# The end of the mixers in a hand-made order, and a first up chunk made of two parts

## The chip, the cores and the metric

The kernel runs on 1 core of one Trainium2 chip. The metric is device time in microseconds (us) of one execution, the median of 3 runs.

## The reference

One inference step of a decoder layer, for 256 prompt tokens and 8 x 4 sampled tokens (288 in all), width 1024, in float32:

```
h   = RMSNorm(x)
p   = h @ w_in                       # columns [q | k | v | B | C | u]
att = rotary q/k, dilated sliding-window attention, 8 heads of 64
cnv = B * causal_depthwise_conv3(C * u)          # 512 channels
mix = concat(RMSNorm(att), RMSNorm(cnv)) @ w_out
x  += RMSNorm(mix)
x  += RMSNorm(relu(RMSNorm(x) @ w_up)^2 @ w_down)
```

Outputs are the new x, the new keys and values, and the convolution's state (the last two rows of C * u, `o_cs` in the kernel).

## The kernel before, in words

**Layout.** Activations lie transposed: 128 channels on the partitions, 288 tokens along a row. A width of 1024 is eight such blocks ("rows" here, index `kc` or `j`). The weights come in 96 chunks, each the eight 128x128 blocks that make 128 output channels: chunks 0 to 7 are q and k, 8 to 11 v, 12 to 23 C, u and B of the convolution, 24 to 31 `w_out` (outputs `mix0` to `mix7`), 32 to 63 `w_up`, 64 to 95 `w_down`. SyncE's queue brings them in blocks of two (`raw`, line 137) into three buffers; a block is requested when the buffer of the third block before it is free.

**Two-part floats.** A float32 product is made of three passes over rounded parts. ACT writes the high part `hi` of a chunk (L164), DVE or POOL the rest `lo` (L165, `split_w`), into three buffers (`splp`) and two more (`spx`). Activations have the same two parts: `mh` and `ml` (attention half `mh0`, `ml0`, convolution half `mh1`, `ml1`), later `hh` and `hl`. `mm3` (L198) issues hi·xh, hi·xl and lo·xh, so that a chunk is 24 matmuls of 288 columns. `take` and `ahead` split a chunk one ahead of its use.

**The end of the mixers.** The gated convolution makes four channel blocks `co`. For the last two, TensorE makes B (chunks 22 and 23), DVE multiplies (`bs2`, `bs3`, then `co`), ACT squares (`sqc`), and `rsqrt_rows` (L205) sums the squares with a matmul (`ss_conv`), takes logarithm and exponential on ACT, and mends the result on DVE (L214, L215, L218). Meanwhile five chunks of `w_out` (`NW = 5`) run over the four rows of the attention half, `mix_half(m, 0, True)`. Then each of the five runs over the convolution half, and mix5, mix6, mix7 are whole chunks. POOL makes `lo24` and `lo25` (`POOL_LO`) and `ml1` of the second convolution row (`POOL_ML`).

**From the mix to the up product.** `post` (L715) squares each mix output (`q_m`, summed in `ssm`) and scales it with the gain of the norm (`mg`). After mix7 comes the norm (`ss_mix`, `y_mix`, `t_mix`, `s1`), and TensorE runs 28 filler matmuls (`warm(WARM1)`, L243) whose result is not used. Then DVE and ACT make row by row mg·s1, the new x, `hh` = x·g and `hl`. Row 0 has a short cut: `gx` = x·g of row 0 and `gm`, which is mix0 times both gains, are made early, and hh0 = gm·s1 + gx. Four up chunks (`NW = 4`) follow the rows as they come; after them each up chunk runs by itself, and `evac_up` (L795 to L798) writes the squared relu into `fh` and `fl`.

**What sets the order.** A scheduler orders the instructions of each engine by the order in which the program text issues them, its estimates, and the hints `after`, `issue_after` and `high_priority`. Inside `manual_schedule` the named engines take the order of the text. Every engine and DMA queue takes its instructions in order; semaphores make it wait for what others write.

Of the kernel before, what the change touches and what calls it, by code (L numbers as in the profile page):

```python
# [108 lines left out]
def layer(ctx, tc, xt, vec, cst, kt, vt, st, wts, o_y, o_k, o_v, o_cs):  # L109
# [483 lines left out]
    def group_norm(src, vcol, c0, c1, hf, ssq, nm, pool, tag):  # L593
        n = c1 - c0
        if mh[hf] is None:
            mh[hf] = act.tile([P, 4, NT], F32R, tag="act", name=f"mh{hf}")
            ml[hf] = act.tile([P, 4, NT], F32R, tag="act", name=f"ml{hf}")
        dh, dl = mh[hf], ml[hf]
        s = nrm.tile([P, NT], F32, tag="s", name=f"s_{nm}")
        if n <= 64:  # L600
            for ch in range(4):
                nc.scalar.mul(src[:, ch, c0:c1], src[:, ch, c0:c1], vv[:, vcol + ch:vcol + ch + 1])
        chain = rsqrt_rows(ssq, m512, n, s[:, :n], nm, pool, tag)
        if n <= 64:
            nc.vector.tensor_mul(src[:, :, c0:c1], src[:, :, c0:c1], s[:, :n].unsqueeze(1).to_broadcast([P, 4, n]))
            nc.scalar.copy(dh[:, :, c0:c1], src[:, :, c0:c1])
            d = nc.vector.tensor_sub(dl[:, :, c0:c1], src[:, :, c0:c1], dh[:, :, c0:c1].bitcast(F32))
            return chain[0], d.ins
        for ch in range(4):
            nc.vector.scalar_tensor_tensor(src[:, ch, c0:c1], src[:, ch, c0:c1], vv[:, vcol + ch:vcol + ch + 1],  # L610
                                           s[:, :n], ALU.mult, ALU.mult)
            nc.scalar.copy(dh[:, ch, c0:c1], src[:, ch, c0:c1])
            e = nc.gpsimd if hf == 1 and ch in POOL_ML else nc.vector
            e.tensor_sub(dl[:, ch, c0:c1], src[:, ch, c0:c1], dh[:, ch, c0:c1].bitcast(F32))
# [42 lines left out]
    group_norm(aT, V_ATT, 0, SEQ, 0, [acc_a[:, 0:SEQ]], "attp", pa, "a")  # L657
# [8 lines left out]
    picks = d_select(1)  # L666
    b2 = conv_b(2, 22, [lambda: [f() for f in picks[0:2]], lambda: [f() for f in picks[2:4]]])
    es.close()
    pt = ctx.enter_context(tc.tile_pool(name="pt", bufs=6, space=PSUM))
    spx = ctx.enter_context(tc.tile_pool(name="spx", bufs=2, side="right"))  # L670
    sqd = cv.tile([P, 4, ND], F32, tag="w", bufs=4, name="sqd")
    acc_d = cv.tile([P, ND], F32, name="acc_d")
    with tc.high_priority():
        nc.scalar.square(sqd, aT[:, :, SEQ:NT])
        d = nc.vector.tensor_reduce(acc_d, sqd.rearrange("p c t -> p t c"), axis=mybir.AxisListType.X, op=ALU.add)
        chain = group_norm(aT, V_ATT, SEQ, NT, 0, [acc_d], "attd", pt, "o")
# [3 lines left out]
    b3 = conv_b(3, 23)  # L680
    sq3 = cv.tile([P, NT], F32, tag="w", bufs=4, name="sqc3")
    with tc.high_priority():
        conv_out(*b3)
# [1 line left out]
        with after(last_mm[0]):
            group_norm(co, V_CONV, 0, NT, 1, [acc_c, sq3], "conv", pt, "o")
    NW = 5
    ws = [take(24, 0)]
    with after(*chain[:1]):
        ws += [take(25, 0)] + [split_w(26 + m, parts=4, pool=spx) for m in range(2)] + [take(28, 0)]  # L690
    pss = []

    def mix_half(m, hf, start):
        if start:
# [1 line left out]
        for j in range(4):
            mm3(pss[m][:, :NT], ws[m], 4 * hf + j, mh[hf][:, j], ml[hf][:, j], start and j == 0, not start and j == 3)

    for m in range(NW):
        mix_half(m, 0, True)  # L700
# [70 lines left out]
    with tc.manual_schedule(engines={mybir.EngineType.DVE, mybir.EngineType.Activation}):  # L771

        nc.vector.tensor_mul(gm, gm, s1)
        nc.vector.tensor_add(hh[0][:, 0], gm, gx)
# [3 lines left out]
        low_h(0)
        for kc in range(2, KC):
            residual(kc)  # L780
            hi_last = high_h(kc)
            low_h(kc - 1)
        lo_last = low_h(7)
        residual(0)
# [16 lines left out]
    pss = [pt.tile([P, 512], F32, tag="o", name=f"up{m}") for m in range(NW)]  # L801
    for kc in range(2):
        for m in range(NW):
            mm_h(pss[m][:, :NT], ws[m], kc, hh[0][:, kc], kc == 0)
        for m in range(NW):
            mm_l(pss[m][:, :NT], ws[m], kc, hl[0][:, kc], False)
    for kc in range(2, KC):
        for m in range(NW):
            mm3(pss[m][:, :NT], ws[m], kc, hh[kc // 4][:, kc % 4], hl[kc // 4][:, kc % 4], False, kc == KC - 1)
# [111 lines left out]
```

## Time and profile before

| | |
|---|---|
| time, median of 3 runs | 380.72 us (380.51 to 380.85) |
| profiled execution, its own time | 380.2 us |
| its span, first to last instruction | 378.4 us |
| mean granted TensorE clock | 0.99 |
| busy: TensorE, weight loads | 363.9 us (96%), 336.3 us (89%) |
| busy: DVE, ACT, POOL | 230.1 us (61%), 195.8 us (52%), 32.1 us (8%) |
| DMA | 76.23 MB, mean 201 GB/s |

The span is one profiled execution, 1.8 us shorter than that execution's own time. PE is TensorE, PEld its weight loads (beside the matmuls), DVE, ACT and POOL are VectorE, ScalarE and GpSimd, SP is SyncE. L205 is line 205 of the kernel before. Matmuls are pipelined, so the durations of neighbours overlap; the distance of their starts is their pace. Names are those of the program without their numbers: `hi` stands for every chunk's high part. A row's bracket tells how long the engine had been idle and what released it.

### The profile page before, as it was taken

What the parts mean: (1) busy time and instruction counts of PE and PEld (TensorE: products, weight loads), DVE (VectorE), ACT (ScalarE), POOL (GpSimd) and SP (SyncE); (2) the same over time, 40 slices, a digit from 0 to 9 for tenths busy, and PEclk for the clock granted to TensorE, in tenths of its full rate; (3) what the DMA queues carried; (4) which work ended last, traced back from release to release, by engine and by line L of the source; (5) the groups of instructions that cost most, each with busy time, mean ns of one, the idle gap of its engine ahead of it and who ended that gap; (6) DMA issues with size and microseconds to landing.
All of it is one profiled execution on the core that took longest, in us unless ns stands there. A gap on an engine that the chain in (4) does not pass through costs nothing.

```text
span 378.4 us, 6776 instructions
## 1 busy us (share of the span) xinstructions
PE 363.9 (96%) x2722; PEld 336.3 (89%) x2722; DVE 230.1 (61%) x421; ACT 195.8 (52%) x368; POOL 32.1 (8%) x58
## 2 busy tenths in 40 slices
PE   8999999999999999999999999999999999999971
PEld 7899688676886899899999999999999999999960
DVE  3889767447394967698876666666434344434417
ACT  5979537343364767355765555555344334433310
POOL 0005100114323300000000000000000000000012
PEclk9999999999999999999999999999999999999996
DMA  7994799987993436504535353535444444542003
GB/s 210 423 407 199 263 408 418 409 322 272 396 395 125 133 107 236 193 3 132 203 112 212 124 197 138 186 149 177 158 164 171 153 181 138 197 129 95 2 0 125
DMA packets 18079, 76.23 MB, mean 201 GB/s; under 512 B 2048, under 2 KB 8448, under 8 KB 11136
## 3 DMA queue, kind: packets, MB, share of 16 engines
q1 hardware_dynamic: 17040, 74.56, 53.3%
q10 hardware_dynamic: 1008, 1.24, 0.9%
q8 instruction: 21, 0.34, 0.4%
q14 instruction: 10, 0.08, 0.1%
HBM read 73.40 MB, written 2.40 MB: 200 GB/s over the span
## 4 chain that ended last, share of the span: by engine, by line
PE 85%; DVE 8%; ACT 2%; DMA 2%; issue 1%; SPq 1%; POOL 1%; DVEq 0%; ACTq 0%; POOLq 0%
PE dn L201 9%; PE dn L203 9%; PE dn L202 9%; PE up L201 8%; PE up L203 8%; PE up L202 8%; PE d L470 3%; PE dpv L514 2%; PE mix L201 2%; PE mix L202 2%; PE mix L203 2%; PE qk L203 2%; DMA raw<-wts 2%; PE qk L201 2%; PE qk L202 2%; PE u L201 1%
## 5 line engine op out<-in xcount | busy, mean ns | idle before, releaser
L165 DVE TENSOR_TENSOR lo<-raw,hi 128x1024 fp32r<-128x1024 f32 (+1 forms) x99 | 112.1, 1140 | 78.1 <-ACT hi L164 77.9
L164 ACT CAST hi<-raw 128x1024 fp32r<-128x1024 f32 (+1 forms) x104 | 97.7, 950 | 97.7 <-PE dn L202 56.6
L201 PE MATMUL dn<-fh,hi 128*128 128x288 f32 x256 | 75.8, 296 | 0.0
L202 PE MATMUL dn<-fl,hi 128*128 128x288 f32 x256 | 75.6, 295 | 0.0
L203 PE MATMUL dn<-fh,lo 128*128 128x288 f32 x256 | 75.3, 294 | 0.0
L202 PE MATMUL up<-hl,hi 128*128 128x288 f32 x248 | 73.4, 296 | 0.0
L201 PE MATMUL up<-hh,hi 128*128 128x288 f32 x248 | 73.1, 296 | 0.0
L203 PE MATMUL up<-hh,lo 128*128 128x288 f32 x248 | 73.0, 294 | 0.0
L203 PEld LDWEIGHTS dn<-fh,lo 128*128 128x128 f32 x256 | 48.2, 188 | 0.0
L202 PEld LDWEIGHTS dn<-fl,hi 128*128 128x128 f32 x256 | 48.1, 188 | 0.0
L201 PEld LDWEIGHTS dn<-fh,hi 128*128 128x128 f32 x256 | 48.0, 188 | 0.0
L203 PEld LDWEIGHTS up<-hh,lo 128*128 128x128 f32 x248 | 46.7, 188 | 0.1
L202 PEld LDWEIGHTS up<-hl,hi 128*128 128x128 f32 x248 | 46.6, 188 | 0.1
L201 PEld LDWEIGHTS up<-hh,hi 128*128 128x128 f32 x248 | 46.4, 187 | 0.0
L795 DVE SCALAR_TENSOR_TENSOR r<-up,s 128x288 f32<-128x288 f32 x32 | 14.2, 456 | 14.1 <-PE up L203 14.0
L834 POOL TENSOR_TENSOR mg<-mg,y_f 128x288 f32<-128x288 f32 x1 | 1.0, 1008 | 232.2 <-ACT y_f L213 232.2
L201 PE MATMUL mix<-mh,hi 128*128 128x288 f32 x64 | 19.3, 302 | 0.0
L202 PE MATMUL mix<-ml,hi 128*128 128x288 f32 x64 | 19.0, 297 | 0.0
L203 PE MATMUL mix<-mh,lo 128*128 128x288 f32 x64 | 18.9, 295 | 0.0
L798 DVE TENSOR_TENSOR fl<-r,fh 128x288 fp32r<-128x288 f32 x32 | 14.0, 451 | 0.0
L797 ACT CAST fh<-r 128x288 fp32r<-128x288 f32 x32 | 13.3, 430 | 0.7
L796 ACT ACTIVATE r<-r 128x288 f32<-128x288 f32 x32 | 13.6, 439 | 0.0
(242 smaller groups left out, 636.3 us busy)
## 6 DMA issues: line engine op xcount, KB each, us to landing
raw<-wts SPq DMA_DIRECT2D x45, 1024.0 KB, 4.9
k<-kt SPq DMA_DIRECT2D x16, 640.0 KB, 11.4
v<-vt SPq DMA_DIRECT2D x9, 1024.0 KB, 11.1
raw<-wts SPq DMA_DIRECT2D x4, 512.0 KB, 8.8
o_y<-mg SPq DMA_DIRECT2D x8, 144.0 KB, 1.8
v<-vt SPq DMA_DIRECT2D x2, 512.0 KB, 11.1
c<-cst SPq DMA_DIRECT2D x1, 838.0 KB, 9.4
...
```

The lines of the kernel that those rows point to most:

```text
L164: a = nc.scalar.copy(hi[:, cs], raw[:, cs])
L165: b = (eng or nc.vector).tensor_sub(lo[:, cs], raw[:, cs], hi[:, cs].bitcast(F32))
L201: nc.tensor.matmul(ps, lhsT=a, rhs=xh, start=start, stop=False)
L202: nc.tensor.matmul(ps, lhsT=a, rhs=xl, start=False, stop=False)
L203: return nc.tensor.matmul(ps, lhsT=lo[:, j * P:(j + 1) * P], rhs=xh, start=False, stop=stop)
L470: nc.tensor.matmul(ps[32 * i:32 * i + 32, 0:n], lhsT=qbd[:, p, 4 * g + i], rhs=t[:, i, 0:n], start=p == 0, stop=p == 3, tile_position=(0, ...
L514: nc.tensor.matmul(dpv[g][32 * i:32 * i + 32], lhsT=pt[:, j, 32 * i:32 * i + 32], rhs=t[i], start=False, stop=j == 4, tile_position=(0, 32 ...
L795: nc.vector.scalar_tensor_tensor(r, ps[:, :NT], 0.0, s2, ALU.max, ALU.mult)
L796: nc.scalar.square(r, r)
L797: nc.scalar.copy(fh[:, m], r)
L798: nc.vector.tensor_sub(fl[:, m], r, fh[:, m].bitcast(F32))
L834: nc.gpsimd.tensor_mul(mg[:, 0], mg[:, 0], y)
```

## The change

On the attention half nothing changes but its order. From the B product of chunk 22 to the last convolution-half matmul of the first five mix chunks, TensorE, DVE and ACT now take the order of the text (`manual_schedule`). In it:

- Every split is whole or in two parts, on DVE (before: quarters for chunks 25 to 28, and POOL for `lo24`, `lo25` and one `ml`).
- mix0 and two rows of mix1 come before the sums `ss_conv`. The convolution half of the five chunks runs row by row over all five for two rows, then chunk by chunk for the last two.
- `hi29` is written before the first square of the mix outputs, and the DMA of `o_cs`, on ACT's queue, is issued behind it.

The fillers after mix7 go. In their place, chunk 32, the first of `w_up`, is computed in two parts from what is known before the norm: since the new x is x + s1·mg, its six rows 0 to 5 (`NS = 6`) give `up0a` = w·(x·g) and `up0b` = w·(mg·g), and up0 = up0a + s1·up0b. Each part has 18 matmuls. Nine run before the sums of the norm, 27 after them. The twelve rows x·g and mg·g get high and low parts on ACT and DVE (`apart`), stored in rows 20 to 31 of `fh` and `fl`. Rows 6 and 7 of chunk 32 run after the norm like before. The order of rows is now 6, 7, 0 to 5, with the short cut (`gx`, `gm`) on row 6. The first block has five up chunks (`NW = 5`), chunk 36 is split before the norm, and two DVE operations on `bs1` put up0 together.

The core of the diff (`rsqrt_rows`, `post`, `residual` and `high_h` stay as they were):

```
-    def group_norm(src, vcol, c0, c1, hf, ssq, nm, pool, tag):
...
+    with tc.manual_schedule(engines={mybir.EngineType.PE, mybir.EngineType.DVE, mybir.EngineType.Activation}):
+        ahead(23)
+        ahead(24)
+        ys = [conv_y(ch) for ch in (2, 3)]
...
+        w25 = high_w(25, splp)
...
+        sq_add(acc_c, co[:, 2], "sqc2", False)
+        low_w(25, w25)
+        b3 = g_in(23, "B3")
+        ws = [take(24, 0), w25] + [high_w(26 + i, spx) for i in range(2)]
+        conv_out(3, b3, ys[1])
...
+        nc.scalar.square(sq3, co[:, 3])
+        ws.append(high_w(28, splp))
+        low_w(26, ws[2])
+        low_w(27, ws[3])
+        low_w(28, ws[4], 0, 512)
...
+        mix_rows(0, 0, range(4))
+        mix_rows(1, 0, range(2))
+        s_c = nrm.tile([P, NT], F32, tag="s", name="s_conv")
+        rsqrt_rows([acc_c, sq3], m512, NT, s_c, "conv", pt, "o")
...
+        mix_rows(1, 0, range(2, 4))
+        for m in range(2, NW):
+            mix_rows(m, 0, range(4))
+        for j in range(2):
+            for m in range(NW):
+                mix_rows(m, 1, [j])
+        for m in range(NW):
+            mix_rows(m, 1, range(2, 4))
+        ahead(29)
...
-    nc.scalar.dma_start(out=o_cs, in_=cst_t)
+    with tc.issue_after(splits[29][0]):
+        nc.scalar.dma_start(out=o_cs, in_=cst_t)
...
+    def apart(i, kc, src):
+        g = vv[:, V_MPRE + kc:V_MPRE + kc + 1]
+        a, b = parts[i][kc], parts[i][NS + kc]
+        nc.scalar.mul(a, src, g)
+        nc.vector.scalar_tensor_tensor(b, src, g, a.bitcast(F32), ALU.mult, ALU.subtract)
+
+    for kc in range(NS):
+        apart(0, kc, x[:, kc])
     for m in range(8):
...
         last = post(ps, m, V_POST, mg[:, m], ssm, "m")
-        if m == 0:
+        if m < NS:
+            apart(1, m, mg[:, m])
+        elif m == NS:
             nc.scalar.mul(gm, ps[:, :NT], vpp)
...
-    rsqrt_rows([ssm, last], m1024, NT, s1, "mix")
-    warm(WARM1, "mix", last)
+    w0 = take(32, 0)
+    apsum = [pt.tile([P, 512], F32, tag="o", name=f"up0{n}") for n in "ab"]
+
+    def product(i, kc):
+        mm3(apsum[i][:, :NT], w0, kc, parts[i][kc], parts[i][NS + kc], kc == 0, i == 1 and kc == NS - 1)
+
+    with tc.manual_schedule(engines={mybir.EngineType.PE}):
+        for kc in range(3):
+            product(0, kc)
+        rsqrt_rows([ssm, last], m1024, NT, s1, "mix")
+        for i, kc in [(0, kc) for kc in range(3, NS)] + [(1, kc) for kc in range(NS)]:
+            product(i, kc)
...
+            if i == 3:
+                nc.vector.tensor_mul(bs1, apsum[1][:, :NT], s1)
...
-    ws = [take(32 + m, 0) for m in range(2)] + [split_w(34 + m, pool=spx) for m in range(2)]
+    ws = [w0, take(33, 0)] + [split_w(34 + m, pool=spx) for m in range(2)] + [take(36, 0)]
     with tc.issue_after(hi_last), tc.issue_after(lo_last):
-        ahead(36)
+        ahead(37)
...
+        if m == 0:
+            with tc.issue_after(lo_last):
+                nc.vector.tensor_add(bs1, ps[:, :NT], bs1)
+            ps = bs1
...
-    NW = 4
...
+    NW = 5
+    pss = apsum[:1] + [pt.tile([P, 512], F32, tag="o", name=f"up{m}") for m in range(1, NW)]
+    for i, kc in enumerate(order):
+        ms = range(0 if kc >= NS else 1, NW)
```

How the instructions stand on two engines. On DVE, around `bs3`, the first product of the last convolution block (`co` in its rows is the output, `t_conv` begins the norm's mending steps). Before:

```order
L591 TENSOR_TENSOR acc_c_1404<-acc_c_1404,sqc2_1613 128x288
L605 TENSOR_TENSOR aT_177<-aT_177,s_attd_1591 128x4x32
L607 TENSOR_TENSOR ml0_1406<-aT_177,mh0_1405 128x4x32
L165 TENSOR_TENSOR lo26_1692<-raw13_258,hi26_1691 128x256
L573 TENSOR_TENSOR bs3_1650<-B3_1624,s0_170 128x288
L165 TENSOR_TENSOR lo26_1692<-raw13_258,hi26_1691 128x256
L574 TENSOR_TENSOR co_670<-bs3_1650,cv3_1616 128x256
L576 TENSOR_TENSOR co_670<-bs3_1650,cv3_1616 128x28
L578 TENSOR_TENSOR co_670<-bs3_1650,cv3_1616 128x4
```

And now:

```order
L697 TENSOR_TENSOR ml0_1406<-aT_177,mh0_1405 128x4x32
L604 TENSOR_TENSOR acc_c_1404<-acc_c_1404,sqc2_1625 128x288
L178 TENSOR_TENSOR lo25_1620<-raw12_256,hi25_1619 128x1024
L586 TENSOR_TENSOR bs3_1660<-B3_1629,s0_170 128x288
L587 TENSOR_TENSOR co_670<-bs3_1660,cv3_1550 128x256
L589 TENSOR_TENSOR co_670<-bs3_1660,cv3_1550 128x28
L591 TENSOR_TENSOR co_670<-bs3_1660,cv3_1550 128x4
L178 TENSOR_TENSOR lo26_1655<-raw13_258,hi26_1654 128x1024
```

The quarters of `lo26` that stood before and behind `bs3` are gone; the whole `lo25`, which was POOL's, stands in front of it, and `lo26` behind the three products.

On ACT, from the mix outputs to the split of chunk 31 (`hi31`), which mix7 multiplies. Before:

```order
L720 ACTIVATE q_m1_1836<-mix1_1734 128x288
L721 ACTIVATE mg_1800<-mix1_1734,vv_95 128x288
L164 CAST hi30_1892<-raw15_262 128x1024
L720 ACTIVATE q_m2_1852<-mix2_1747 128x288
L721 ACTIVATE mg_1800<-mix2_1747,vv_95 128x288
L720 ACTIVATE q_m3_1868<-mix3_1760 128x288
L721 ACTIVATE mg_1800<-mix3_1760,vv_95 128x288
L164 CAST hi31_1925<-raw15_262 128x1024
L720 ACTIVATE q_m4_1884<-mix4_1773 128x288
```

And now (`fh` is the high part of a row of x·g or mg·g):

```order
L162 CAST hi30_1890<-raw15_262 128x1024
L767 ACTIVATE gx_1846<-x_94,vv_95 128x288
L775 ACTIVATE fh_1842<-x_94,vv_95 128x288 x6
L756 ACTIVATE ssm_1844<-mix0_1673 128x288
...
L775 ACTIVATE fh_1842<-mg_1841,vv_95 128x288 x2
...
L757 ACTIVATE mg_1841<-mix4_1677,vv_95 128x288
L756 ACTIVATE q_m5_1919<-mix5_1894 128x288
L775 ACTIVATE fh_1842<-mg_1841,vv_95 128x288
L757 ACTIVATE mg_1841<-mix5_1894,vv_95 128x288
L162 CAST hi31_1925<-raw15_262 128x1024
L775 ACTIVATE fh_1842<-mg_1841,vv_95 128x288
```

`hi31` stood behind the scaled copy of mix3; it now stands behind that of mix5, with `gx`, the six copies of x and five of `mg` ahead of it.

On ACT, further on, from mix7 to the logarithm of the norm (`y_mix`). Before:

```order
L164 CAST hi32_2054<-raw16_264 128x1024
L164 CAST hi33_2058<-raw16_264 128x1024
L720 ACTIVATE q_m6_1954<-mix6_1929 128x288
L721 ACTIVATE mg_1800<-mix6_1929,vv_95 128x288
L720 ACTIVATE q_m7_1983<-mix7_1958 128x288
L721 ACTIVATE mg_1800<-mix7_1958,vv_95 128x288
L212 ACTIVATE y_mix_1994<-ss_mix_1991,epsc_120 128x288
```

And now:

```order
L162 CAST hi32_1992<-raw16_264 128x1024
L162 CAST hi33_2087<-raw16_264 128x1024
L162 CAST hi34_2091<-raw17_266 128x1024
L162 CAST hi35_2095<-raw17_266 128x1024
L756 ACTIVATE q_m7_1984<-mix7_1959 128x288
L757 ACTIVATE mg_1841<-mix7_1959,vv_95 128x288
L162 CAST hi36_2099<-raw18_268 128x1024
L221 ACTIVATE y_mix_2012<-ss_mix_2009,epsc_120 128x288
```

`hi34` and `hi35`, which stood ahead of mix5's square, and `hi32` and `hi33` now stand directly ahead of the square of mix7, and `hi36` between that and the logarithm.

## Rows read from the trace of the kernel before

**Rows 1.** The page's busy time of each engine (share of the span, instructions)

```profile
PE 363.9 (96%) x2722; PEld 336.3 (89%) x2722; DVE 230.1 (61%) x421; ACT 195.8 (52%) x368; POOL 32.1 (8%) x58
```

**Rows 2.** TensorE's waits: us in total, times, longest

```profile
PE up L196 <- DVE hl L767: 0.4, 1, 0.4
```

**Rows 3.** TensorE's timeline: start us, us, instruction, count, idle before and releaser

```profile
128.96 0.75 PE L209 MATMUL ss_conv<-sqc,m 128*128 128x288 f32 x2 [0.85 <-ACT sqc L684]
129.68 0.29 PE L202 MATMUL mix<-ml,hi 128*128 128x288 f32 x1
...
153.53 0.65 PE L209 MATMUL ss_mix<-ssm,m 128*128 128x288 f32 x2
...
154.78 3.29 PE L243 MATMUL warm_mix<-q_m,m 128*128 128x128 f32 x28
158.47 0.40 PE L192 MATMUL up<-hh,hi 128*128 128x288 f32 x1 [0.40 <-DVE hh L774]
...
162.42 0.56 PE L201 MATMUL up<-hh,hi 128*128 128x288 f32 x3
```

**Rows 4.** Timeline of POOL and DVE while `lo25` is split

```profile
123.70 3.25 POOL L165 TENSOR_TENSOR lo<-raw,hi 128x256 fp32r<-128x256 f32 x4 [3.23 <-ACT hi L164]
126.28 0.95 DVE L165 TENSOR_TENSOR lo<-raw,hi 128x256 fp32r<-128x256 f32 x1
127.52 0.41 DVE L165 TENSOR_TENSOR lo<-raw,hi 128x256 fp32r<-128x256 f32 x1
```

**Rows 5.** ACT's timeline

```profile
10.48 0.96 ACT L236 ACTIVATE xh<-x,vv 128x288 fp32r<-128x288 f32 x2
...
137.60 1.05 ACT L164 CAST hi<-raw 128x1024 fp32r<-128x1024 f32 x1 [0.37 <-PE mix L202]
138.55 0.41 ACT L720 ACTIVATE ssm<-mix 128x288 f32<-128x288 f32 x1
138.85 0.49 ACT L721 ACTIVATE mg<-mix,vv 128x288 f32<-128x288 f32 x1
139.24 0.50 ACT L742 ACTIVATE gm<-mix,vpp 128x288 f32<-128x288 f32 x1
...
143.99 1.05 ACT L164 CAST hi<-raw 128x1024 fp32r<-128x1024 f32 x1 [0.65 <-PE mix L202]
...
153.73 0.41 ACT L720 ACTIVATE q_m<-mix 128x288 f32<-128x288 f32 x1 [1.58 <-PE mix L203]
...
154.98 0.50 ACT L212 ACTIVATE y_mix<-ss_mix,epsc 128x288 f32<-128x288 f32 x1 [0.45 <-PE ss_mix L209]
...
159.31 0.54 ACT L756 ACTIVATE hh<-x,vv 128x288 fp32r<-128x288 f32 x1 [3.35 <-DVE x L753]
...
168.87 0.78 ACT L760 ACTIVATE q_x<-x 128x288 f32<-128x288 f32 x2
```

**Rows 6.** DVE's timeline

```profile
145.07 1.23 DVE L165 TENSOR_TENSOR lo<-raw,hi 128x1024 fp32r<-128x1024 f32 x1 [1.52 <-ACT hi L164]
146.71 2.36 DVE L165 TENSOR_TENSOR lo<-raw,hi 128x1024 fp32r<-128x1024 f32 x2
...
155.99 0.46 DVE L214 SCALAR_TENSOR_TENSOR t_mix<-y_mix 128x288 f32<-128x288 f32 x1 [2.92 <-ACT y_mix L213]
```

**Rows 7.** The page's DMA issues: count, KB each, us to landing

```profile
raw<-wts SPq DMA_DIRECT2D x45, 1024.0 KB, 4.9
...
o_cs<-cst_t ACTq DMA_DIRECT2D x1, 36.0 KB, 1.5
```

**Rows 8.** SyncE's timeline: the request for chunks 36 and 37

```profile
146.33 0.33 SPq L137 DMA_DIRECT2D raw<-wts  x1
```

**Rows 9.** The tail in TensorE's timeline

```profile
366.28 0.65 PE L842 MATMUL sum<-x,ident 128*128 128x288 f32 x2
...
371.81 1.33 PE L847 MATMUL sum<-mg,ident 128*128 128x288 f32 x2 [4.88 <-DVE mg L845]
```

**Rows 10.** Windows of the tail: busy (count) PE PEld DVE ACT POOL, clock, DMA

```profile
371.00:372.00 1.00, 0.19 (x1) 0.19 (x2) 1.00 (x2) 0.00 (x0) 1.00 (x2) 0.52 0.20 70
```

More of the change, by code (lines that the diff above doesn't have):

```diff
@@ L169, in layer, with raw_of, high_w, low_w @@
     splits = {}
+    def raw_of(s):
+        return blocks[s // 2][:, (s % 2) * 1024:(s % 2) * 1024 + 1024]
+    def high_w(s, pool):
+        w = [pool.tile([P, 1024], F32R, tag=n, name=f"{n}{s}") for n in ("hi", "lo")]
+        nc.scalar.copy(w[0], raw_of(s))
+        return w
+    def low_w(s, w, a=0, z=1024):
+        nc.vector.tensor_sub(w[1][:, a:z], raw_of(s)[:, a:z], w[0][:, a:z].bitcast(F32))
     def after(*ins):
@@ L181, in ahead @@
         if s < 96 and s not in ready:
-            ready[s] = split_w(s, parts=4 if s in (1, 2) or 25 <= s <= 28 else 1, eng=nc.gpsimd if s in POOL_LO else None)
+            ready[s] = split_w(s, parts=4 if s in (1, 2) else 1)
     def take(s, n=1):
@@ L591, in sq_add, with prompt_norm @@
             (e or nc.vector).tensor_add(acc, acc, t[:, :n])
-    def group_norm(src, vcol, c0, c1, hf, ssq, nm, pool, tag):
[L594 to L608, printed above, removed]
-        for ch in range(4):
[L610 to L614, printed above, removed]
+    def prompt_norm():
+        for i in range(2):
+            mh[i] = act.tile([P, 4, NT], F32R, tag="act", name=f"mh{i}")
+            ml[i] = act.tile([P, 4, NT], F32R, tag="act", name=f"ml{i}")
+        s = nrm.tile([P, NT], F32, tag="s", name="s_attp")
+        rsqrt_rows([acc_a[:, 0:SEQ]], m512, SEQ, s[:, :SEQ], "attp", pa, "a")
+        for ch in range(4):
+            a, h = aT[:, ch, 0:SEQ], mh[0][:, ch, 0:SEQ]
+            nc.vector.scalar_tensor_tensor(a, a, vv[:, V_ATT + ch:V_ATT + ch + 1], s[:, :SEQ], ALU.mult, ALU.mult)
+            nc.scalar.copy(h, a)
+            nc.vector.tensor_sub(ml[0][:, ch, 0:SEQ], a, h.bitcast(F32))
     v_chunk(0)
@@ L656, in layer @@
     acc_c = cv.tile([P, NT], F32, tag="acc", name="acc_c")
[L657 removed]
+    prompt_norm()
     conv_c(3, 20)
@@ L665, in layer @@
         sq_add(acc_c, co[:, ch], f"sqc{ch}", ch == 0, nc.gpsimd)
[L666 to L676, printed above, removed]
@@ L677, in layer @@
-    with after(chain[0], d.ins):
-        conv_out(*b2)
-        sq_add(acc_c, co[:, 2], "sqc2", False)
[L680 to L683, printed above, removed]
-        nc.scalar.square(sq3, co[:, 3])
[L685 to L690, printed above, removed]
@@ L691, in layer, with mix_rows @@
-    pss = []
-    def mix_half(m, hf, start):
-        if start:
-            pss.append((pg if m < 2 else pt).tile([P, 512], F32, tag="g" if m < 2 else "o", name=f"mix{m}"))
[L696 to L700, printed above, removed]
+    ahead(22)
+    NW = 5
+    pss = []
+    def mix_rows(m, hf, js):
+        for j in js:
+            mm3(pss[m][:, :NT], ws[m], 4 * hf + j, mh[hf][:, j], ml[hf][:, j], hf == 0 and j == 0, hf == 1 and j == 3)
@@ L771, in layer @@
     with tc.manual_schedule(engines={mybir.EngineType.DVE, mybir.EngineType.Activation}):
+        order = list(range(NS, KC)) + list(range(NS))
         nc.vector.tensor_mul(gm, gm, s1)
-        nc.vector.tensor_add(hh[0][:, 0], gm, gx)
-        residual(1)
-        hi_last = high_h(1)
+        nc.vector.tensor_add(hh[NS // 4][:, NS % 4], gm, gx)
+        residual(order[1])
+        hi_last = high_h(order[1])
         nc.vector.tensor_add(gx, gm, gx)
[L778 to L784, printed above, removed]
-    ws = [take(32 + m, 0) for m in range(2)] + [split_w(34 + m, pool=spx) for m in range(2)]
+        low_h(NS)
+        for i in range(2, KC):
+            residual(order[i])
+            hi_last = high_h(order[i])
+            low_h(order[i - 1])
+            if i == 3:
+                nc.vector.tensor_mul(bs1, apsum[1][:, :NT], s1)
+        lo_last = low_h(order[7])
+        residual(NS)
+    ws = [w0, take(33, 0)] + [split_w(34 + m, pool=spx) for m in range(2)] + [take(36, 0)]
     with tc.issue_after(hi_last), tc.issue_after(lo_last):
-        ahead(36)
+        ahead(37)
         for kc in range(KC):
@@ L798, in evac_up @@
         nc.vector.tensor_sub(fl[:, m], r, fh[:, m].bitcast(F32))
-    NW = 4
[L801 to L809, printed above, removed]
+    NW = 5
+    pss = apsum[:1] + [pt.tile([P, 512], F32, tag="o", name=f"up{m}") for m in range(1, NW)]
+    for i, kc in enumerate(order):
+        ms = range(0 if kc >= NS else 1, NW)
+        a, b = hh[kc // 4][:, kc % 4], hl[kc // 4][:, kc % 4]
+        for m in ms:
+            mm_h(pss[m][:, :NT], ws[m], kc, a, i == 0 and m > 0)
+            if i > 1:
+                mm_l(pss[m][:, :NT], ws[m], kc, b, i == (KC - 1 if m else KC - NS - 1))
+        if i < 2:
+            for m in ms:
+                mm_l(pss[m][:, :NT], ws[m], kc, b, m == 0 and i == KC - NS - 1)
     for m in range(NW, 32):
         w = take(32 + m)
-        ps = (pg if m == 6 else pt).tile([P, 512], F32, tag="g" if m == 6 else "o", name=f"up{m}")
+        ps = (pg if m == 5 else pt).tile([P, 512], F32, tag="g" if m == 5 else "o", name=f"up{m}")
         last = gemm(ps, w, hh, hl)
```

51 lines of the change are left out of this document (41 added, 10 removed).

## The prediction

> **What bounds the kernel now.** I read the busy shares first. TensorE is busy for 363.9 of 378.4 us [rows 1], so a change can win only where TensorE stands, or where it does work that can go. I then read TensorE's waits: inside the stretch that the change touches they are short, such as 0.4 us for the first low part of the up product [rows 2]. The timeline shows the others [rows 3]: 0.85 us for the conv square before `ss_conv`; and from 154.78 to 158.47 TensorE does only the filler `warm_mix`, while the norm of the mix output runs on ACT and DVE. The reader is to see there also the pace: from the second matmul after the conv wait, 129.68, to the last norm, 153.53, stand 179 matmuls of 288 columns, 0.1333 us each. A chunk (24 of them) costs 3.20 us, so mix4 ended at 143.94 and mix6 at 150.33.
>
> The other engines are asked only for what must be ready. ACT's timeline [rows 5] gives prices by start-to-start time: 0.95 for a `hi` cast of 1024 columns (137.60 to 138.55), 0.30 for a square out of PSUM, 0.39 for a scaled copy out of PSUM. Two scaled copies from SBUF, `xh<-x,vv`, take 0.96 and one alone 0.54, so each further one costs 0.42. ACT takes its instructions in the written order.
>
> **Part 1, the end of the mixers.** The wait of 0.85 us at 128.96 [rows 3] has its cause on DVE: `sqc3` needs the last conv output, and DVE reached it late, behind quarter splits. One of these took 0.95 us while POOL was splitting lo25 (123.70 to 126.95), the next 0.41 [rows 4]. The change takes lo24, lo25 and one `ml` from POOL and puts them whole on DVE. That is 1.18 us for each `lo` (two in 2.36, [rows 6]): lo24 goes into DVE's idle time before `om`, lo25 stands directly before `bs3`. DVE loses the slowed quarter and its halves around `bs3`, so `bs3` starts at about the same time. TensorE gets six matmuls more to do before it needs `sqc3` (two rows of mix1), 6 x 0.1333 = 0.80 us, nearly the wait's length. I take 0.80 us gained here. Bounds: 0, if lo25 holds `bs3` back, for which mix1 now waits because it reuses its PSUM buffer; 1.1, if POOL's silence shortens the small DVE operations as well. The nearest row is the wait itself. In after's second half the chunks go side by side, and each ends six matmuls (0.80) after the one before: mix0 at 139.94, mix2 at 141.54, mix4 at 143.14, mix6 at 149.54.
>
> **Part 2, what ACT now has before hi31.** Here the price lies. Before, mix0 to mix4 ended 1.6 us apart and ACT did each chunk's square and scaled copy as it came; hi31 started at 143.99, as soon as its buffer came free [rows 5]. In the new row order hi31 stands behind everything that chunks 0 to 5 leave on ACT. Followed by price: the square of mix2 starts 0.2 us after mix2 ends (the latency of the square of mix7, 153.53 to 153.73 [rows 3, 5]), at 141.74; hi30 at 142.04; `gx` at 142.99. (`gx` also waits for `o_cs`, now issued behind hi29; hi29 can start at 139.94, so with 1.5 us to landing [rows 7] it is there by 142.4.) From `gx` to hi31 stand 12 scaled copies from SBUF (`gx`, six parts of x, five of `mg`): 12 x 0.42 = 5.04; six `mg`: 6 x 0.39 = 2.34; four squares: 4 x 0.30 = 1.20. The sum is 8.58, so hi31 starts at 151.57 and ends 1.05 later, at 152.62. DVE's lo31 takes 1.23 [rows 6]: 153.89.
>
> TensorE is through with mix6 at 149.54. It stands until 152.6, does the two matmuls that need hi31 alone, and stands again until 153.93 for lo31. The 22 matmuls left of mix7 end at 156.86, where 152.74 was to be had. That is a stand of 4.1 us, new and not in any row of before.
>
> The same queue goes on. From hi31's start 0.95; part 5 0.42; the square of mix6 0.30; `mg` and `gm` 0.78; hi32 to hi35 4 x 0.95 = 3.80: the square of mix7 starts at 157.82, though mix7 was over at 156.86. After it and `mg` (0.69) stands hi36, at 158.51. Its block (chunks 36 and 37) is requested only when lo31 has released the buffer (before: lo31 ended at 146.30, the request went out at 146.33 [rows 6, 8]), so at 153.9, and lands 4.9 later [rows 7], at 158.8. hi36 ends at 159.88, lo36 then holds DVE for 1.18, and only behind it stands the norm's first DVE step `t_mix`: 161.1 against 155.99 [rows 6]. The logarithm and exponential on ACT (159.8 to 160.8) are ready before that. From `t_mix` to the first up matmul were 2.48 us before (155.99 to 158.47), the same steps now: 163.6. So TensorE gets there 5.1 us later.
>
> **Part 3, the two-part first up chunk.** It adds 36 matmuls ahead of that point, in place of the 28 fillers. Nine run from 156.86 to 158.1, before the norm's sums (about 1.2 us), 27 after these, to about 163: hidden whole. Of the 768 up matmuls (32 chunks), 18 need not run after the norm: 18 x 0.1333 = 2.40 us won. If they were not hidden (a norm that came back as early as before) up to 1.2 us of them would show. The first two rows serve five chunks instead of four, 15 matmuls instead of 12. Before, the first 24 matmuls (3.20) took from 158.47 to 162.42 [rows 3], 0.75 us lost; now one wait of some 0.4 for the first `hl` is left: 0.3 won. The two additions on `bs1` (0.46 each at `t_mix`'s price) lie on DVE beside TensorE, which needs 1.6 us for a row of twelve where DVE needs about 1.3. Were that cover gone they would cost 0.9.
>
> **Sum.** +5.1 - 2.4 - 0.3 = +2.4 us, the 0.8 of part 1 being inside the 5.1. Against the profiled execution's own 380.2 us that is 382.6. Its 380.2 is 0.5 below the median of the runs, 380.72, so I forecast **383.1 us**.
>
> Bounds of the terms. The twelve scaled copies may cost 0.34 (two squares `q_x` from SBUF take 0.78, one 0.44) to 0.54 (one alone): -1.0 to +1.4 us. I keep 0.42, the same operation with the same shapes. Part 1: +0.8 to -0.3. A landing of the block 0.5 us later or earlier moves `t_mix` by +0.5 or -0.3, the queue on ACT being then last.
>
> **The clock.** In the tail TensorE stands for 4.88 us; there the granted clock falls from 1.00 to 0.52, that is from 2.4 to 1.2 GHz, and the same pair of matmuls takes 1.33 instead of 0.65 us [rows 9, 10]. The new stand is 3.1 us, two matmuls, 1.0 us. No row of before has one of that length. If the clock fell there, the 22 matmuls of mix7 would cost 2.9 us more; 0.8 of that hides, because ACT takes up mix7's square only 0.8 us after it may. The Trainium skill (TensorE: Matmul & The Clock Gate, Part 1) says that half rate is the array's default and full rate is held only while the array is busy; by that rule the removal of the fillers and this stand speak against the change, and the sum would be the rival's below, not mine.
>
> **Rivals.**
> - ACT keeps up (faster). If hi31 were ready at 149.5, mix7 would end at 152.74, nine products and the sums would end at about 155.2, `t_mix` would start some 0.2 us after 155.99, and 2.7 us are won: 378.2 us. It decides at 6.5 us for the list that I price at 8.58 (142.99 to 149.54): the scaled copies would have to cost 0.25 each. No ACT row of 288 columns is below 0.30. For it speaks only that one execution's profile was read. Chance 0.13.
> - Gain and stand cancel. Copies at 0.34, POOL's silence worth the full 1.1, the block early: 2.4 - 1.0 - 0.3 - 0.3 = +0.8, about 381.4, and a little less is no change. Chance 0.09.
> - The clock falls in the stand: +2.4 + 2.1 = +4.5, 385.2 us. Chance 0.17.
> - My forecast, hi31 late at full clock: 382.0 to 384.5, chance 0.61.
>
> **How the numbers follow.** A measurement of this kernel can tell about 0.2%, 0.76 us, from no change. Faster by more than that: the first rival, 0.13. No change: 0.09. Slower: 0.61 + 0.17 = 0.78. The range must leave out no more than the first rival and part of the second, so it runs from 381.2 to 385.5: from just below the second rival's edge over the forecast's own bounds to the clock rival.
>
> **What would show it.** Right: in the waits of TensorE a new row of some 3 us, `mix` waiting for ACT's `hi`, and one of about 1 us for DVE's `lo`, both at mix7; ACT without a pause from about 143 to 158; the first up matmul of the new rows at about 163.6; no wait for `sqc3` near 128; a granted clock of 1.00 throughout the stand. Wrong: mix7 following mix6 without a gap, or hi31's cast at about 144 to 147; then the queue on ACT is mis-sized and the time is below 380. Part 3 is wrong if TensorE is still on `up0b` when the first `hh` is ready, part 1 if mix1 waits long for `bs3`.

## The result and the profile after

The changed kernel takes 383.67 us, median of 6 runs (382.87 to 384.72), against 380.67 us before (6 runs): a ratio of 1.008, 95% interval [1.007, 1.009]. It is slower by 3.0 us. The forecast was 383.1 us, with a range from 381.2 to 385.5.

The profiled execution is the longest of the six: 384.72 us, span 382.9, that is 4.5 more than the span before. The loss lies between 149 and 166 us. The page's busy times, to be read against [rows 1]: TensorE works 2.2 us more inside a span that is 4.5 us longer.

```profile
PE 366.1 (96%) x2712; PEld 338.5 (88%) x2712; DVE 236.8 (62%) x431; ACT 198.4 (52%) x364; POOL 27.8 (7%) x52
```

TensorE's waits (us in total, times, longest), to be read against [rows 2]. Two waits at mix7 are new, one for ACT's `hi`, one for DVE's `lo`. None is left for the conv square.

```profile
PE mix L210 <- ACT hi L162: 3.0, 1, 3.0
PE mix L212 <- DVE lo L163: 0.6, 1, 0.6
```

TensorE's timeline, against [rows 3] (start us, us, instruction, idle before and releaser):

```profile
129.37 0.65 PE L218 MATMUL ss_conv<-sqc,m 128*128 128x288 f32 x2
...
149.66 0.29 PE L212 MATMUL mix<-mh,lo 128*128 128x288 f32 x1
152.98 0.46 PE L210 MATMUL mix<-mh,hi 128*128 128x288 f32 x1 [3.02 <-ACT hi L162]
153.23 0.44 PE L211 MATMUL mix<-ml,hi 128*128 128x288 f32 x1
154.24 0.61 PE L212 MATMUL mix<-mh,lo 128*128 128x288 f32 x1 [0.56 <-DVE lo L163]
...
159.68 0.44 PE L210 MATMUL up0a<-fh,hi 128*128 128x288 f32 x1
...
165.46 0.29 PE L212 MATMUL up0b<-fh,lo 128*128 128x288 f32 x1
165.68 0.40 PE L201 MATMUL up0a<-hh,hi 128*128 128x288 f32 x1
```

The reader is to see three things. The sums `ss_conv` follow without the 0.85 us of before. mix7 begins 3 us late and its matmuls then start 0.24 us apart, not 0.133. The first matmul of the new rows comes at 165.68, 7.2 us later than the 158.47 of [rows 3]; the span grew by 4.5, so 2.7 us were won behind that point.

ACT's timeline, against [rows 5]. The cast at 140.28 is `hi29`, ahead of which ACT was idle for 2.45 us; the cast at 151.84 is `hi31`. From 142.0 to there ACT was busy without a pause.

```profile
140.28 1.05 ACT L162 CAST hi<-raw 128x1024 fp32r<-128x1024 f32 x1 [2.45 <-PE mix L211]
...
143.24 0.54 ACT L767 ACTIVATE gx<-x,vv 128x288 f32<-128x288 f32 x1
143.68 2.66 ACT L775 ACTIVATE fh<-x,vv 128x288 fp32r<-128x288 f32 x6
...
151.84 1.09 ACT L162 CAST hi<-raw 128x1024 fp32r<-128x1024 f32 x1
...
159.92 0.41 ACT L756 ACTIVATE q_m<-mix 128x288 f32<-128x288 f32 x1 [1.71 <-PE mix L212]
160.23 0.50 ACT L757 ACTIVATE mg<-mix,vv 128x288 f32<-128x288 f32 x1
160.61 1.05 ACT L162 CAST hi<-raw 128x1024 fp32r<-128x1024 f32 x1
```

DVE's timeline, against [rows 6]: `lo31`, `lo36`, and `t_mix`, 7.2 us later than its 155.99 there.

```profile
152.96 1.22 DVE L163 TENSOR_TENSOR lo<-raw,hi 128x1024 fp32r<-128x1024 f32 x1 [0.81 <-ACT hi L162]
...
161.69 1.23 DVE L163 TENSOR_TENSOR lo<-raw,hi 128x1024 fp32r<-128x1024 f32 x1 [1.65 <-PE ss_mix L218]
163.20 0.46 DVE L223 SCALAR_TENSOR_TENSOR t_mix<-y_mix 128x288 f32<-128x288 f32 x1 [0.28 <-ACT y_mix L222]
```

The windows view by half microseconds (length, then busy us and count of PE, PEld, DVE, ACT, POOL, the granted clock, DMA share, GB/s). The clock falls to 0.50 (1.2 GHz) at about 153.2, just behind the stand, which ended at 152.98, and comes back to 1.00 (2.4 GHz) at 160.

```profile
152.50:153.00 0.50, 0.02 (x1) 0.03 (x1) 0.04 (x1) 0.50 (x2) 0.00 (x0) 1.00 0.00 0
153.00:153.50 0.50, 0.50 (x2) 0.32 (x2) 0.50 (x1) 0.50 (x2) 0.00 (x0) 0.68 0.00 0
153.50:154.00 0.50, 0.17 (x1) 0.00 (x0) 0.50 (x1) 0.50 (x3) 0.00 (x0) 0.50 0.00 0
...
159.50:160.00 0.50, 0.50 (x4) 0.50 (x4) 0.50 (x1) 0.08 (x1) 0.00 (x0) 0.50 0.56 213
160.00:160.50 0.50, 0.50 (x6) 0.50 (x6) 0.04 (x1) 0.50 (x2) 0.00 (x0) 1.00 1.05 442
```

### The profile page after: what moved, and what is told of

Read it like the earlier page. It is cut to its first block, busy times and chain, and to the rows that moved or that the text cites. A ratio compares the mean times of both kernels' runs of the same rounds, so it can differ in the third digit from the quotient of the medians.

```text
span 382.9 us, 6760 instructions
## 1 busy us (share of the span) xinstructions
PE 366.1 (96%) x2712; PEld 338.5 (88%) x2712; DVE 236.8 (62%) x431; ACT 198.4 (52%) x364; POOL 27.8 (7%) x52
## 4 chain that ended last, share of the span: by engine, by line
PE 84%; DVE 8%; ACT 2%; DMA 2%; issue 1%; SPq 1%; POOL 0%; DVEq 0%; POOLq 0%
PE dn L210 9%; PE dn L212 9%; PE dn L211 9%; PE up L210 7%; PE up L212 7%; PE up L211 7%; PE d L479 3%; PE dpv L523 2%; PE mix L212 2%; DMA raw<-wts 2%; PE qk L212 2%; PE mix L211 2%; PE mix L210 2%; PE qk L210 2%; PE qk L211 2%; PE C L210 1%
## 5 line engine op out<-in xcount | busy, mean ns | idle before, releaser
L163 DVE TENSOR_TENSOR lo<-raw,hi 128x1024 fp32r<-128x1024 f32 x88 | 108.6, 1239 | 78.8 <-ACT hi L162 77.1
L162 ACT CAST hi<-raw 128x1024 fp32r<-128x1024 f32 x88 | 92.2, 1054 | 96.3 <-PE dn L211 56.7
L210 PE MATMUL up<-hh,hi 128*128 128x288 f32 x216 | 63.9, 296 | 0.0
L212 PE MATMUL up<-hh,lo 128*128 128x288 f32 x216 | 63.7, 295 | 0.0
L211 PE MATMUL up<-hl,hi 128*128 128x288 f32 x216 | 63.7, 295 | 0.0
L212 PEld LDWEIGHTS up<-hh,lo 128*128 128x128 f32 x216 | 40.7, 188 | 0.1
L211 PEld LDWEIGHTS up<-hl,hi 128*128 128x128 f32 x216 | 40.5, 188 | 0.0
L210 PEld LDWEIGHTS up<-hh,hi 128*128 128x128 f32 x216 | 40.5, 187 | 0.1
L210 PEld LDWEIGHTS mix<-mh,hi 128*128 128x128 f32 x64 | 13.0, 203 | 3.3 <-ACT hi L162 3.3
L212 PEld LDWEIGHTS mix<-mh,lo 128*128 128x128 f32 x64 | 13.1, 205 | 0.9 <-DVE lo L163 0.9
```

Of the source, the lines that this page charges most:

```text
L163: b = nc.vector.tensor_sub(lo[:, cs], raw[:, cs], hi[:, cs].bitcast(F32))
L210: nc.tensor.matmul(ps, lhsT=a, rhs=xh, start=start, stop=False)
L211: nc.tensor.matmul(ps, lhsT=a, rhs=xl, start=False, stop=False)
L212: return nc.tensor.matmul(ps, lhsT=lo[:, j * P:(j + 1) * P], rhs=xh, start=False, stop=stop)
```

## Experiments

Theory: ACT's queue puts `hi31` behind the two-part chunk's copies, TensorE stands at mix7, and what follows shifts. First rival: the mixers' own order loses. Second: the two-part chunk is too dear in any order. A third question is what the slow clock costs.

### e1: the mixers' order alone

Behind the mixers stands the code of before (in outline):

```
-    parts = ...   (and apart, product, bs1)
+    warm(WARM1, "mix", last)
-    NW = 5
+    NW = 4
```

> The changed kernel with the two-part first up chunk undone: the hand-made order of the mixers stays, the rest (fillers after mix7, four up chunks, rows 0 to 7) is that of the kernel before. My theory: the loss sits in the queue that the two-part chunk puts on ACT, and the mixers' order alone wins the 0.8 us of the conv-square wait: 379.9 us, no wait for hi31 above 0.3 us, t_mix near 155.2. Rival: the mixers' order itself loses (the conv half row by row ends the first five chunks late): 382 us or more, with a wait at mix7.

Measured: 379.40 us against 380.54, ratio 0.9968 [0.9958, 0.9979]: faster by 1.14 us. ACT's timeline has `hi31`, the first of three casts, at 147.64:

```profile
147.64 3.03 ACT L162 CAST hi<-raw 128x1024 fp32r<-128x1024 f32 x3
```

DVE's timeline has `t_mix` at 155.57:

```profile
155.57 0.46 DVE L223 SCALAR_TENSOR_TENSOR t_mix<-y_mix 128x288 f32<-128x288 f32 x1 [0.63 <-ACT y_mix L222]
```

TensorE does not wait at mix7. The first rival falls: the order wins, and the two-part chunk on top of it costs 4.3 us.

### e2: hi31 in time, nothing taken from ACT

```
+    ahead(30)
+    ahead(31)
     for kc in range(NS):
         apart(0, kc, x[:, kc])
```

> The changed kernel with hi30 and hi31 issued ahead of the copies of x times gain; hi32 to hi36 then stand behind mix7's square by the scheduler's order. My theory: ACT has too much to do as a whole, not only in the wrong order: mix7 follows mix6 without a gap, but up0a then waits some 3 us for hi32, and y_mix stands behind hi33 to hi36 (from about 159.4): 382 to 383.5 us. Rival A: only hi31's place matters: the 3.6 us of stand and the slow clock after it go, 377 to 378.5 us. Rival B: the norm waits for hi36 and its block in any case: 383.7, no change.

Measured: 383.12 us, ratio 1.0067 [1.0054, 1.0079]. mix7 runs through at full clock; in TensorE's timeline the next wait stands at `up0a`:

```profile
155.28 0.37 PE L210 MATMUL up0a<-fh,hi 128*128 128x288 f32 x1 [2.81 <-issue]
156.50 0.45 PE L212 MATMUL up0a<-fh,lo 128*128 128x288 f32 x1 [0.71 <-DVE lo L163]
```

Its `hi32` is, in ACT's timeline, the first of five casts behind mix7's square:

```profile
154.06 4.91 ACT L162 CAST hi<-raw 128x1024 fp32r<-128x1024 f32 x5
```

The view names "issue" as the releaser; the cast that ends at about 155.1 is what `up0a` multiplies with. So far the theory held: with `hi31` in time, `hi32` is late. Its second half did not: ACT was through with `hi36` at 158.97, and `y_mix` waited for TensorE's sums, because behind the two waits the clock was 0.50 from 156.7 to 160.1 here too. DVE, though, was busy with the five `lo` until 160.99, so that `t_mix`, at 161.33, could not have come much earlier at full clock. ACT's timeline, then DVE's:

```profile
160.32 0.50 ACT L221 ACTIVATE y_mix<-ss_mix,epsc 128x288 f32<-128x288 f32 x1 [1.35 <-PE ss_mix L218]
```

```profile
155.22 5.77 DVE L163 TENSOR_TENSOR lo<-raw,hi 128x1024 fp32r<-128x1024 f32 x5 [1.89 <-ACT hi L162]
```

### e3: three rows in two parts

```
-NS = 6
+NS = 3
```

> The changed kernel with three rows in two parts instead of six: six scaled copies fewer on ACT, 18 matmuls in parts instead of 36. My theory: five copies fewer ahead of hi31 and gm more, so hi31 starts 1.8 us earlier, near 150.0; the stand at mix7 falls to about 1.3 us for hi31 and 1 us for lo31, the clock stays at 1.00, t_mix near 159.5; nine matmuls less are won: 382 to 383 us. Rival: the copies are not what hi31 waits for, the stand stays at 3 us: 384.5 or more, because less is won.

Measured: 383.49 us, ratio 1.0079 [1.0066, 1.0091], above the forecast. `hi31` comes at 149.65, the waits at mix7 fall to 1.3 and 0.7 us at full clock, and `t_mix` comes at 159.10, all as expected. But with 18 products in place of the fillers TensorE runs out of work, as its timeline shows:

```profile
161.58 0.61 PE L201 MATMUL up0a<-hh,hi 128*128 128x288 f32 x1 [2.95 <-DVE hh L836]
161.98 0.44 PE L202 MATMUL up0a<-hh,lo 128*128 128x288 f32 x1
162.22 0.44 PE L201 MATMUL up<-hh,hi 128*128 128x288 f32 x1
```

It stands 2.95 us, the clock falls to 0.50 from about 160.9 to 167.7, and 0.24 us per matmul eats what was gained. I had left out what the fillers were there for.

### e4 and e5: the stand filled

```
-            gemm(ps, w, mh, ml)
+            if m == 7:
+                with tc.manual_schedule(engines={mybir.EngineType.PE}):
+                    fil = pt.tile([P, 512], F32, tag="o", name="fil")
+                    for _ in range(26):    # e5: range(13)
+                        nc.tensor.matmul(fil[:, 0:P], lhsT=m1024, rhs=m1024, start=True, stop=True)
+                    gemm(ps, w, mh, ml)
+            else:
+                gemm(ps, w, mh, ml)
```

> The changed kernel with 26 filler matmuls of 128 columns (0.1175 us each, 3.06 us) between mix6 and mix7, where TensorE stood; their result is not used. My theory: the granted clock stays at 1.00, mix7's 22 last matmuls take 2.9 us instead of 5.3, t_mix comes near 161.1 and the time falls by about 2 us below the changed kernel, to 381.6 to 382.3. Rival: the slow clock costs nothing on the path, since ACT and the block of chunk 36 are late in any case: 383.7, no change.

Measured: 383.61 us, ratio 1.0081 [1.0067, 1.0095]. This one was mis-sized: TensorE's timeline shows 52 matmuls where 26 were issued.

```profile
149.39 5.97 PE L790 MATMUL fil<-m 128*128 128x128 f32 x52
```

mix7 then began 2.1 us later than in the changed kernel, so the run can't tell the two apart. It shows only that the clock stays at 1.00 over a filled stand.

> The filled stand again, with half the fillers: each filler issued shows as two matmuls in the trace, so that 26 took 5.97 us and pushed mix7 2.1 us later than the change does; 13 fill the 3 us that were empty. Theory: the clock stays at 1.00, mix7 ends near 157.0 instead of 159.7, but hi36 waits for its block (requested when lo31 ends at about 154.1, 4.9 us to landing), so t_mix comes at about 161.4 instead of 163.2: 382.5 to 383.2 us. Rival: the whole 2.7 us come through: 381.0 to 381.6.

Measured: 382.70 us, ratio 1.0053 [1.0039, 1.0067]. The fillers fill the stand, and the clock stays at 1.00 there and through mix7, as the windows show (columns as above):

```profile
152.00:154.00 2.00, 1.14 (x9) 0.71 (x7) 1.28 (x2) 2.00 (x5) 0.00 (x0) 1.00 0.00 0
154.00:156.00 2.00, 2.00 (x15) 2.00 (x16) 1.56 (x3) 2.00 (x4) 0.00 (x0) 1.00 0.51 98
```

In ACT's timeline `hi36` waits 0.30 us for its block:

```profile
159.00 1.05 ACT L162 CAST hi<-raw 128x1024 fp32r<-128x1024 f32 x1 [0.30 <-DMA raw<-wts]
```

`t_mix` comes at 161.22 in DVE's:

```profile
161.22 0.45 DVE L223 SCALAR_TENSOR_TENSOR t_mix<-y_mix 128x288 f32<-128x288 f32 x1
```

So the slow clock costs about 1.0 us of the median (the two intervals leave some 0.4 to 1.7), and 2.2 us are lost without it. Behind a faster mix7 the block's landing is next.

### e6: the two-part chunk alone, on the mixers of before

The edit against the changed kernel, in outline:

```
-    with tc.manual_schedule(engines={PE, DVE, Activation}):   (end of mixers)
+    (group_norm, conv_b, mix_half, POOL_LO, POOL_ML as before)
```

> The two-part first up chunk alone, on the mixers of the kernel before (quarter splits, POOL's share, chunk by chunk). Theory: what hurts is both together. Here the first chunks end one after the other from 137.5 on, x copies and hi29 start some 2 us earlier, and ACT reaches mix7's square at about 155, 1 us late: -2.4 of work, -0.3, +0.9: 378.5 to 379.8 us. Rival: twelve copies and one more split are too much for ACT in any order: 382 us or more.

Measured: 379.79 us against 380.50, ratio 0.9978 [0.997, 0.9987]: faster by 0.7 us. ACT's timeline shows why: with `o_cs` long gone, `gx` and the six copies run ahead of everything else, and `hi31` is there in time (the cast at 147.19). From the conv square to the norm TensorE stands only twice: 0.83 us for that square, as before, and 0.63 us for `lo29`.

```profile
137.19 0.54 ACT L731 ACTIVATE gx<-x,vv 128x288 f32<-128x288 f32 x1 [0.57 <-DVE ml L614]
137.63 2.67 ACT L739 ACTIVATE fh<-x,vv 128x288 fp32r<-128x288 f32 x6
...
147.19 1.08 ACT L164 CAST hi<-raw 128x1024 fp32r<-128x1024 f32 x1
```

The second rival falls too. Each half of the change wins (1.14 and 0.7 us); together they lose 3.0.

### e9 and e10: which edit of the mixers holds ACT up

e9 sends `o_cs` out early, e10 ends mix0 to mix2 ahead of mix3 and mix4:

```
-    with tc.issue_after(splits[29][0]):
-        nc.scalar.dma_start(out=o_cs, in_=cst_t)
+    nc.sync.dma_start(out=o_cs, in_=cst_t)                      # e9
...
-        for j in range(2):
-            for m in range(NW):
-                mix_rows(m, 1, [j])
-        for m in range(NW):
-            mix_rows(m, 1, range(2, 4))
+        for rows in (range(2), range(2, 4)):                    # e10
+            for m in range(3):
+                mix_rows(m, 1, rows)
+        for m in range(3, NW):
+            mix_rows(m, 1, range(4))
```

> The changed kernel with one edit undone: o_cs goes out as soon as its rows are copied (on SyncE's queue ahead of raw15) instead of behind hi29 on ACT's. Theory: gx and four x copies then fill ACT's idle time in front of hi29 (137.9 to 140.3), the list ahead of hi31 gets about 2 us shorter, the stands at mix6 and mix7 fall to 2.5 to 3 us together without a fall of the clock, and t_mix comes near 158.5 to 159.5 instead of 163.2: 379.7 to 381.0 us. Rival: the row order of the conv half is the cause and o_cs next to nothing: 383 us or more.

Measured: 383.20 us, ratio 1.0061 [1.0045, 1.0077]. By the median the rival holds; by the trace, both were off. The six executions spread from 381.93 to 383.81 us. The copies did move ahead of `hi29` (from 138.22), and `hi31` came 2.5 us earlier, at 149.30. But in the scheduler's order `hi30` slid behind the scaled copy of mix4, and the wait moved to mix6, with the slow clock behind it (TensorE's timeline):

```profile
148.38 0.40 PE L210 MATMUL mix<-mh,hi 128*128 128x288 f32 x1 [1.81 <-ACT hi L162]
...
149.64 0.61 PE L212 MATMUL mix<-mh,lo 128*128 128x288 f32 x1 [0.63 <-DVE lo L163]
150.05 0.44 PE L210 MATMUL mix<-mh,hi 128*128 128x288 f32 x1
```

> The changed kernel with the conv half of mix0 to mix2 ended first, then mix3 and mix4 whole, instead of row by row over all five; o_cs stays behind hi29. Theory: mix0 ends and hi29 starts 1.6 us earlier, the same list follows, hi31 starts near 150.0, the stand at mix7 falls to about 2.5 us, t_mix near 159.5: 380.8 to 381.8 us. Rival: o_cs is the whole cause and the row order next to nothing: 383 us or more.

Measured: 381.30 us, ratio 1.002 [1.0011, 1.003]: 2.4 us less than the changed kernel by this edit alone. `hi29` starts at 138.38, `hi31` at 149.94, TensorE waits 1.44 and 0.73 us at full clock in the traced execution, and `t_mix` comes at 159.50, as forecast. `hi29` and `hi31` in ACT's timeline, the waits in TensorE's, `t_mix` in DVE's:

```profile
138.38 1.05 ACT L162 CAST hi<-raw 128x1024 fp32r<-128x1024 f32 x1 [0.98 <-PE mix L211]
...
149.94 1.09 ACT L162 CAST hi<-raw 128x1024 fp32r<-128x1024 f32 x1
```

```profile
151.09 0.40 PE L210 MATMUL mix<-mh,hi 128*128 128x288 f32 x1 [1.44 <-ACT hi L162]
...
152.35 0.40 PE L212 MATMUL mix<-mh,lo 128*128 128x288 f32 x1 [0.73 <-DVE lo L163]
```

```profile
159.50 0.45 DVE L223 SCALAR_TENSOR_TENSOR t_mix<-y_mix 128x288 f32<-128x288 f32 x1
```

Of the edits undone one at a time, the row order over five chunks costs most: it makes the first three chunks end late, and close together.

### e7, e8 and e11: versions that join the gains

All three take e9's and e10's edits, `ahead(30)` as in e2, and overlap the conv norm's rows (`conv_norm(0)` and `conv_norm(1)` ahead of the first `ml`). e8 keeps six rows; e11 has `NS = 4`; e7 has `NS = 3`, four up chunks, `ahead(36)` behind the norm, and `warm(8, "mix")` behind the products.

> A version made from what the first four runs showed: the hand-made mixers, with the conv half of mix0 to mix2 ended first (138.4 instead of 140.0), the conv norm's rows overlapped, o_cs on SyncE's queue ahead of raw15, hi30 ahead of the copies, three rows in two parts, four up chunks in the first block, 8 fillers issued behind the products. Theory: ACT reaches mix7's square in time, t_mix at 155 to 156, nine matmuls and half of the short waits are won: 378.0 to 378.8 us. Rival: the queue on ACT is still late at hi31 or hi33: 380 us or more.

> The same mixers and early x copies as in the run before this one, but with the change's six rows, five up chunks and chunk 36 ahead of the norm, no fillers. Theory: hi31 at about 148.1, a stand of 0.9 us for lo31, hi36 waits for its block (requested at 150.4) and t_mix comes near 157.6, against 155.6 with the mixers alone; -2.7 of work: 378.3 to 379.5 us. Rival: the row order of the conv half is not what made ACT late, hi31 stays at 151 or later: 382 us or more.

> The last version (mixers with early chunk ends, x copies and o_cs early) with four rows in two parts and five up chunks in the first block. Theory: four copies fewer bring hi31 to 146.5, no stand at mix7, hi36 at about 153.7, t_mix near 156.1 instead of 157.4; six matmuls (0.8 us) less are won: 378.2 to 378.8 us. Rival: the stand before hh grows to 2 us or more and the clock falls there: 379.5 us or more.

| run | us | ratio to before, 95% | `hi31` cast | `t_mix` | longest wait, mix7 to the first `hh` |
|---|---|---|---|---|---|
| e7 | 378.97 | 0.9959 [0.9946, 0.9971] | 145.72 | 156.39 | 0.5 |
| e8 | 378.89 | 0.9956 [0.9943, 0.9968] | 147.97 | 157.43 | 0.6 |
| e11 | 378.56 | 0.9948 [0.9933, 0.9962] | 146.36 | 156.17 | 1.5 |

The lowest, e11, is 2.2 us faster than before and 5.1 us faster than the changed kernel; the three intervals overlap, so the runs do not rank the three versions. In ACT's timeline of e11 `hi31` is cast before mix7 needs it, and in TensorE's the only wait left from mix7 to the first `hh` is the one for `hh`:

```profile
146.36 1.09 ACT L162 CAST hi<-raw 128x1024 fp32r<-128x1024 f32 x1
```

```profile
158.66 0.40 PE L201 MATMUL up0a<-hh,hi 128*128 128x288 f32 x1 [1.54 <-DVE hh L838]
```

e7 came out at 378.97, above its 378.0 to 378.8: `t_mix` came 0.4 us behind its 155 to 156, and with twelve matmuls for each of the first rows, as in the kernel before, TensorE still waited 0.5 us for `hh` and 0.5 for the first `hl`. e8 is 2.4 us below e10; what the early `o_cs`, the place of `hi30` and the overlap of the norm's rows each give of that was not measured.

### e12: a second execution of the changed kernel

> The changed kernel once more, unchanged, for the trace of a second execution: the profiled one took 384.7 us, the other five 382.9 to 383.9. Theory: all of them have the 3 us stand at mix7, but the slow clock begins and ends at other moments, so that a shorter part of mix7 runs at half clock; this trace has the stand, a slow stretch of another length than 153.0 to 160.0, and t_mix earlier or later by what that stretch saves: 382.9 to 384.7 us. Rival: the slow stretch is the same to 0.2 us and the difference lies elsewhere, for example at the start.

Measured: 383.87 us (5 runs), ratio 1.0086 [1.0072, 1.01]. The traced execution took 384.1 us. In its windows the clock falls inside the stand and is back at 158.8, both 1.2 us earlier than in the first trace:

```profile
151.50:152.00 0.50, 0.00 (x0) 0.00 (x0) 0.41 (x1) 0.50 (x2) 0.00 (x0) 0.98 0.00 0
152.00:152.50 0.50, 0.00 (x0) 0.00 (x0) 0.00 (x0) 0.50 (x1) 0.00 (x0) 0.50 0.00 0
...
158.50:159.00 0.50, 0.50 (x4) 0.50 (x4) 0.50 (x2) 0.00 (x0) 0.00 (x0) 0.69 1.20 164
159.00:159.50 0.50, 0.50 (x6) 0.50 (x5) 0.50 (x1) 0.14 (x1) 0.00 (x0) 1.00 0.55 147
```

The stand is the same, 3.03 us. Against the theory the slow stretch is no shorter; it lies 1.2 us earlier, so that the last matmuls of mix7 run at full clock. `t_mix` comes at 162.54 instead of 163.20, but 0.24 of these 0.66 us were there before the stand (`hi31` at 151.60 instead of 151.84). What the place of the slow stretch explains between these two executions is about 0.4 us.

## Why the prediction came out right, and where it did not

**Part 1.** The wait for the conv square is gone, as forecast. mix6, which ended at 150.33 before and was forecast at 149.54, ended at 149.79 in the first trace and at 149.54 in that of e12. Alone, the mixers' order is worth 1.14 us (e1), the upper bound that was named.

**Part 2, the queue on ACT.** The step held to a few tenths: `hi31` forecast at 151.57, measured 151.84; `lo31`'s end 153.89, measured 154.18; the first stand 3.1, measured 3.02; the second 1.0, measured 0.56. The view counts that wait from the end of the matmul before, which was already slow (0.44 us); at full clock, in e10, it shows 0.73. In e5, which takes the clock away from the sum, `hi36` waits for its block as forecast, `t_mix` comes at 161.22 where 161.1 was forecast, and the time is 2.2 us above before, where the sum said 2.4.

**Part 3.** The gain of 2.4 + 0.3 was 2.7 us (7.2 late at the first matmul, 4.5 at the end of the span). All 36 products were hidden. In this trace the last began at 165.46, when `hh` was about to end, at 165.63: with a norm any faster they would have shown. At full clock there was room, 0.74 us of waiting for `hh` in e5.

**The clock.** This is the step that failed: "hi31 late at full clock" had a chance of 0.61 and the fall of the clock 0.17. The clock fell, in both traced executions. In the others it very likely fell too: their mean granted clock is 0.980 to 0.984, that of all executions of e1, e5 and e6 0.987 to 0.992. The 22 matmuls of mix7 took 5.44 us (154.24 to 159.68) instead of 2.93. For the profiled execution the rival's sum is exact: +4.5 us of span, `t_mix` at 161.1 + 2.1 = 163.2. That is partly luck: mix7 lost 2.5 us, not the 2.9 of the prediction, `lo31` ended 0.3 late, and `t_mix` stood 0.28 us behind the end of `lo36` for `y_mix`, where the prediction had `lo36` last. It is also the longest execution. Against e5 `t_mix` is 2.0 us late in this trace and 1.3 in that of e12, and the clock's share of the median is about 1.0 us, not 2.1. So the median, 383.67, lies between the forecast, 383.1, and that rival, 385.2. That it fell into the band of "hi31 late at full clock" (382.0 to 384.5) is luck, since the clock was not full. In the windows the clock falls to 0.50 inside the stand of 3.03 us (e12) or 0.2 us behind that of 3.02 us, and with fillers in the stand it stays at 1.00 (e4, e5). By the rule of the Trainium skill (TensorE: Matmul & The Clock Gate, Part 1), half rate is the default and full rate is held only while the array is busy, so a fall was to be reckoned with, and these traces agree. The forecast gave more weight to the lack of such a row in the trace of before.

**What the prediction did not see.** It priced the queue as a whole and did not ask which edit makes it late. The runs show that neither part loses by itself (e1, e6). The row order alone accounts for 2.4 of the 3.0 us (e10). ACT is idle for 2.45 us ahead of `hi29`, and its work is crowded behind it. That the late `o_cs` has a share is shown by the trace of e9 (copies move ahead of `hi29`, `hi31` comes 2.5 us earlier), hardly by its time (0.5 us less), since the wait moved to mix6.
